# The first matmul of two MLPs as seven half-sized products per 512 hidden columns, with weight sums on VectorE and in accumulating transfers

## The chip, the cores and the metric

One NeuronCore of a Trainium2 chip runs the whole program; the other cores are idle. The metric is the time of one execution on the device in microseconds (us). Five engines work from their own instruction lists: TensorE (PE in the profile, its weight loads PEld), VectorE (DVE), ScalarE (ACT), GpSimd (POOL) and SyncE (SP). SP and POOL issue the transfers (DMAs); only those of POOL add to what lies at the destination (`accum_op=ALU.add`).

## The reference

Two layers on 512 tokens of width 1024, in float32. Each layer is a token mixer (dilated window attention in the first, latent attention in the second) and then an MLP with a hidden width of 4096. The change is about the MLP:

```python
def sq_relu_mlp(h, w1, w2):
    a = jax.nn.relu(h @ w1)
    return (a * a) @ w2

for i in range(DEPTH):
    ...
    x = x + y
    h = rms_norm(x, norm_ffn[i])
    x = x + sq_relu_mlp(h, ffn_w1[i], ffn_w2[i])
```

## The kernel before

Every float32 operand is split in two parts in TensorE's fp32r format: ACT copies it to `hi`, DVE subtracts to get `lo`. A product is then three matmuls: hi·hi, hi·lo and lo·hi. So each weight block costs an ACT copy and a DVE subtraction besides the matmuls.

The MLP stands in `mlp`. `up(ch, grp)` makes 512 of the 4096 hidden columns: four weight units of 128x1024 (`raw`, three buffers, loaded by SP at L147 and split at L157 and L158), 96 matmuls of 512 columns each at L185, and Relu and Square on ACT (L891, L892) into `a2`. Only the first group of a layer runs its matmuls in halves of 256 columns, 192 of them. The normalized tokens stand in `hT_m` as hi and lo, written by `norm_tile` (L228 on ACT, L229 on DVE) while `project`, the output projection of the mixer, still runs for later token tiles.

`down(ch)` takes 1024 hidden columns, in `wino`: seven products in the manner of Strassen and Winograd in place of eight, each of 24 matmuls of 512 columns (L852). Its weight sums need no engine: SP loads a block into a slot of `wqs` (L783) and POOL adds another to it (L781). The sums of the activations are DVE's (L789, into two buffers `S`), their splits L757 and L758 (into four buffers `asp`), and the results are added to the residual at L826. `wqs` takes the space of the big tile `hT` of the mixer, and so waits for the last matmul of `project`.

The order of calls is up(0,0), up(0,1), then for each of three chunks up(ch+1,0), down(ch), up(ch+1,1), and last down(3). A scheduler of the tile framework decides the order on each engine from these calls by its own estimates, and it places waits where a buffer is reused. An engine and a queue work strictly in their order. In the first layer the last `down` also runs the norm for the next mixer, `done0`: its tiles `xn` use the tag and the two buffers of `S`.

Two other places are touched. In the first mixer, `both(4, bT[g], ...)` needs a sum of weights that DVE adds (`add_block`, L334). In the second, the scores (L1114) of the last head pairs run beside the start of `project`.

Of the kernel before, what the change touches and what calls it, by code (L numbers as in the profile page):

```python
# [17 lines left out]
P = 128  # L18
# [69 lines left out]
def encoder_kernel(ctx: ExitStack, tc: tile.TileContext, x, norm_mix, norm_ffn, a_w_qkv, a_q_gain, a_k_gain,  # L88
# [218 lines left out]
    def v_phase(vp):  # L307
# [139 lines left out]
        def piece(g, ba):  # L447
# [11 lines left out]
            add_block(bT[g], bT[g], b21[g])  # L459
# [295 lines left out]
    def split_a(x, pool):  # L755
        t = pool.tile([P, 4, 2, 256], F32R, tag="asp", name=nm("asp"), bufs=4)
        A.activation(t[:, :, 0], x, AF.Copy)  # L757
        V.tensor_tensor(t[:, :, 1], x, t[:, :, 0].bitcast(F32), op=ALU.subtract)  # L758
        return t

    def wino(tag, Aq, w, wqs, pool, resid, done=None):
# [24 lines left out]
        def stmp(name, x, y, op):  # L786
            if name not in S:
                S[name] = pool.tile([P, 4, 256], F32, tag="S", name=nm("S"), bufs=2)
            V.tensor_tensor(S[name], x, y, op=op)  # L789
            return S[name]  # L790
# [14 lines left out]
        b7 = fetch(s7, (1, 1), add=True)  # L805

        def operands(p):
            if p == 5:
                return stmp("c", Aq(1, 0), Aq(1, 1), ALU.subtract), bT
            if p == 1:  # L810
                return Aq(0, 0), b1
            if p == 3:
                stmp("d", S["c"], Aq(0, 0), ALU.subtract)
                return stmp("c", S["d"], Aq(0, 1), ALU.add), b3
            if p == 6:
                return S["d"], fetch(sT, (1, 1), add=True)
            if p == 7:
                return stmp("c", Aq(0, 0), Aq(1, 0), ALU.subtract), b7
# [10 lines left out]

        banks = {}  # L830
        for p, chain, first, (i, n, op) in ORDER if done is None else ORDER_LAST:
            a, wq = operands(p)
            at = split_a(a, pool)
# [20 lines left out]
            put(i, n, op, bk)  # L854


    SLOTS = [(0, 1, 2, 3)]
    for _ in range(3):
# [3 lines left out]
    ORDER = [(1, "a", True, (0, 0, ALU.add)), (5, "b", True, (1, 1, ALU.add)), (3, "b", False, (0, 1, ALU.add)),  # L862
             (6, "a", False, (0, 1, ALU.subtract)), (2, "d", True, (0, 0, ALU.add)),
             (7, "a", False, (1, 1, ALU.subtract)), (4, "a", False, (1, 0, ALU.add))]

    ORDER_LAST = [ORDER[0], ORDER[4]] + ORDER[1:4] + ORDER[5:]

    def mlp(layer, w1, w2, hT_m, resid, pool, done):
        a2s = {}

        wqs = big.tile([P, 8, 2, 512], F32, tag="hT", name=nm("wqs"))

        def up(ch, grp):
            if grp == 0:
                if ch % 2:
                    a2s[ch] = pool.tile([P, 8, S], F32, tag="a2", name=nm("a2"))
                else:
                    a2s[ch] = x16.tile([P, 8, S], F32, tag="x16", name=nm("a2"))
            a2 = a2s[ch]
            c0 = ch * 1024 + grp * 512  # L880
            first = c0 == 0

            def mm(o, kt, hi, lo, hv, n=256 if first else 512):
                wh, wl = hi[:, o * P:(o + 1) * P], lo[:, o * P:(o + 1) * P]
                sl = slice(hv * n, hv * n + n)
                hh, hl = hT_m[:, kt, 0, sl], hT_m[:, kt, 1, sl]
                return [(wh, hh, sl), (wh, hl, sl), (wl, hh, sl)]

            def evac(o, acc):
                f = grp * 4 + o  # L890
                A.activation(a2[:, f], acc, AF.Relu)  # L891
                A.activation(a2[:, f], a2[:, f], AF.Square)  # L892

            run_block(w_units(w1, c0, 512), [4] if first else [1] * 4, 512, mm, evac, halves=2 if first else 1)

        def down(ch):
            a2 = a2s.pop(ch)
            wino(layer * 4 + ch, lambda i, j: a2[:, 4 * j:4 * j + 4, 256 * i:256 * i + 256],
# [4 lines left out]
        for ch in range(3):  # L903
            up(ch + 1, 0)
            down(ch)
            up(ch + 1, 1)
# [320 lines left out]
```

## Time and profile before

| | us |
|---|---|
| median of 3 runs | 1429.62 (1429.39 to 1430.68) |
| the profiled execution | 1427.53 |
| its span in the trace | 1425.8 |

The profiled execution is 2.1 us below the median; its span leaves out 1.7 us around the program.

The page of the profile has the busy time of each engine, the span in 40 slices, the DMA queues, and the chain of work that ended last. It is read here in that order, and then by windows of the trace: the stretch from 549 to 882 us is the MLP of the first layer, and that from 1087 to the end is the MLP of the second. A row of a group of instructions gives line, engine, operation, tile written and read, shape, count, busy time, mean duration in ns and the idle time ahead of it. A row of a window gives its length and the busy time of PE, PEld, DVE, ACT and POOL with their counts, then the granted clock, the share of the DMA engines, and GB/s. A row of the chain gives start, length, engine, tile, line and count. In a row of DMA issues the last number is the median from issue to landing.

| DMA queue | packets | MB | share of 16 engines |
|---|---|---|---|
| SP (q1) | 101808 | 144.96 | 31.6% |
| POOL (q0) | 19184 | 39.07 | 15.2% |

### The profile page before, as it was taken

How to read it: one execution, taken by the hardware profiler on the slowest of the kernel's cores; microseconds unless marked ns; L12 is line 12 of the kernel's file. 1: busy time of each engine (PE TensorE's matmuls, PEld its weight loads, DVE VectorE, ACT ScalarE, POOL GpSimd, SP SyncE). 2: the span in 40 equal slices, each digit the busy share in tenths (PEclk: the TensorE clock that was granted, in tenths of full speed). 3: DMA queues.
4: the chain of work that ended last, by engine and by line, in shares of the span. 5: the costliest groups of instructions: out<-in, count | busy, mean ns of one | idle time of the engine just before them, and what ended most of it. 6: DMA issues, size and time to landing. Idle time of an engine off the chain costs nothing.

```text
span 1425.8 us, 19234 instructions
## 1 busy us (share of the span) xinstructions
PE 1394.0 (98%) x7044; PEld 1183.8 (83%) x7044; DVE 939.6 (66%) x1497; ACT 740.5 (52%) x1594; POOL 217.2 (15%) x240
## 2 busy tenths in 40 slices
PE   7999999999999999999999999999999999999998
PEld 7999888988888988888888887777768888888886
DVE  6886768676886754465564759788745365575647
ACT  6554656464564623553545446677633553544543
POOL 1110212021112001020010203433201020020201
PEclk9999999999999999999999999999999999999999
DMA  9535222322322335668493844200115658394835
GB/s 323 166 134 168 75 87 87 107 89 75 118 61 77 121 134 195 174 133 222 116 233 99 206 120 91 82 31 30 44 40 163 183 127 231 93 234 128 192 90 118
DMA packets 121086, 185.25 MB, mean 130 GB/s; under 512 B 8416, under 2 KB 58336, under 8 KB 120992
## 3 DMA queue, kind: packets, MB, share of 16 engines
q1 hardware_dynamic: 101808, 144.96, 31.6%
q0 software_dynamic: 19184, 39.07, 15.2%
q8 instruction: 55, 0.90, 0.3%
q14 instruction: 39, 0.32, 0.1%
HBM read 176.13 MB, written 7.86 MB: 129 GB/s over the span
## 4 chain that ended last, share of the span: by engine, by line
PE 89%; DVE 6%; ACT 2%; issue 1%; DMA 1%; POOL 0%; SPq 0%; DVEq 0%; ACTq 0%; POOLq 0%
PE acc L185 51%; PE sc L852 11%; PE tp L852 7%; PE tp L124 4%; PE sc L421 3%; PE acc L1138 1%; PE sc L1032 1%; PE acc L1114 1%; PE tp L421 1%; DVE wlo L796 1%; PE sco L701 1%; PE sc L587 1%; PE acc L421 1%; PE sco L697 1%; DVE wlo L407 1%
## 5 line engine op out<-in xcount | busy, mean ns | idle before, releaser
L185 PE MATMUL acc<-whi,hT 128*128 128x512 f32 (+2 forms) x1216 | 384.2, 390 | 2.2 <-ACT hT L739 1.3
L185 PE MATMUL acc<-hT_f,whi 128*128 128x512 f32 (+1 forms) x1152 | 318.7, 366 | 1.7 <-DVE resid L915 1.2
L158 DVE TENSOR_TENSOR wlo<-raw,whi 128x1024 fp32r<-128x1024 f32 (+3 forms) x146 | 172.4, 1189 | 180.2 <-ACT whi L157 179.9
L185 PEld LDWEIGHTS acc<-whi,hT 128*128 128x128 f32 x1216 | 225.4, 188 | 42.0 <-ACT hT L739 1.9
L185 PEld LDWEIGHTS acc<-hT_f,whi 128*128 128x128 f32 x1152 | 208.1, 189 | 37.4 <-DVE resid L915 1.6
L185 PE MATMUL acc<-wlo,hT 128*128 128x512 f32 (+2 forms) x608 | 235.9, 388 | 0.0
L157 ACT ACTIVATE whi<-raw 128x1024 fp32r<-128x1024 f32 (+3 forms) x146 | 149.7, 1031 | 161.5 <-PE acc L185 64.1
L796 DVE TENSOR_TENSOR wlo<-wqs,whi 128x1024 fp32r<-128x1024 f32 x112 | 137.9, 1232 | 113.4 <-ACT whi L795 113.4
L185 PE MATMUL acc<-hT_f,wlo 128*128 128x512 f32 (+1 forms) x576 | 204.9, 366 | 0.0
L795 ACT ACTIVATE whi<-wqs 128x1024 fp32r<-128x1024 f32 x112 | 118.8, 1061 | 161.3 <-PE acc L185 65.8
L852 PE MATMUL sc<-whi,asp 128*128 128x512 f32 x512 | 164.9, 390 | 0.8 <-DVE resid L826 0.7
L781 POOL DMA_DIRECT2D wqs<-in_ffn_w_dram x64 | 77.6, 1344 | 546.1 <-DVE wlo L796 362.4
L185 PEld LDWEIGHTS acc<-wlo,hT 128*128 128x128 f32 x608 | 114.4, 188 | 18.7 <-issue 0.2
L185 PEld LDWEIGHTS acc<-hT_f,wlo 128*128 128x128 f32 x576 | 108.5, 189 | 17.4
L852 PE MATMUL tp<-whi,asp 128*128 128x512 f32 x352 | 112.2, 390 | 1.8 <-DVE resid L826 1.8
L852 PEld LDWEIGHTS sc<-whi,asp 128*128 128x128 f32 x512 | 96.1, 188 | 21.4 <-issue 1.5
L132 POOL TENSOR_TENSOR qrs<-rs_v,nhalf 128x4 f32<-128x4 f32 x48 | 58.7, 1228 | 288.8 <-DVE rs_v L129 239.7
L852 PE MATMUL sc<-wlo,asp 128*128 128x512 f32 x256 | 99.6, 389 | 0.0
L137 ACT ACTIVATE junk<-acc 128x128 f32<-128x128 f32 x192 | 53.0, 276 | 56.4 <-PE acc L185 51.4
L852 PEld LDWEIGHTS tp<-whi,asp 128*128 128x128 f32 x352 | 66.1, 188 | 16.4 <-DVE resid L826 2.7
L852 PE MATMUL tp<-wlo,asp 128*128 128x512 f32 x176 | 68.2, 389 | 0.0
L295 ACT ACTIVATE qkT<-tp 128x512 f32<-128x512 f32 x48 | 35.8, 765 | 51.2 <-PE tp L124 50.9
(231 smaller groups left out, 2185.3 us busy)
## 6 DMA issues: line engine op xcount, KB each, us to landing
wqs<-in_ffn_w_dram SPq DMA_DIRECT2D x80, 512.0 KB, 5.1
raw<-in_ffn_w_dram SPq DMA_DIRECT2D x64, 512.0 KB, 4.5
wqs<-in_ffn_w_dram POOLq DMA_DIRECT2D x64, 512.0 KB, 7.5
raw<-in_a_w_qkv_dram SPq DMA_DIRECT2D x96, 256.0 KB, 3.1
b<-in_a_w_qkv_dram SPq DMA_DIRECT2D x24, 384.0 KB, 5.7
vall<-vo POOLq DMA_DIRECT2D x24, 192.0 KB, 2.2
raw<-in_a_w_o_dram SPq DMA_DIRECT2D x8, 512.0 KB, 3.8
raw<-in_b_w_o_dram SPq DMA_DIRECT2D x8, 512.0 KB, 3.7
```

Of the source, the lines that this page charges most:

```text
L124: PE.transpose(o, i, ident)
L132: G.tensor_tensor(out, v[:, :n], nhalf[:, :n], op=ALU.pow)
L137: A.activation(junk, x, AF.Square, scale=1.0 / math.sqrt(dim), accum_out=out)
L157: A.activation(hi[:, :nk, :n], raw[:, :nk, :n], AF.Copy)
L158: V.tensor_tensor(lo[:, :nk, :n], raw[:, :nk, :n], hi[:, :nk, :n].bitcast(F32), op=ALU.subtract)
L185: PE.matmul(accs[o][:, oc], lhsT=lt, rhs=rt, start=(kt == 0 and p_i == 0 and hv == 0), stop=(kt == total - 1 and p_i == 2), skip_group_che ...
L295: A.activation(dst, tv, AF.Copy)
L421: PE.matmul(banks[t][:, :VH], lhsT=lt, rhs=rt[:, j], start=(first and k == 0 and i_ == 0), stop=(k == 3 and i_ == 2), skip_group_check=True)
L781: marks["sum"] = nc.gpsimd.dma_start(t, src, accum_op=ALU.add).ins
L795: A.activation(hi, x, AF.Copy)
L796: V.tensor_tensor(lo, x, hi.bitcast(F32), op=ALU.subtract)
L852: PE.matmul(bk[t], lhsT=lt, rhs=rt[:, j], start=(first and k == 0 and i_ == 0), stop=(k == 3 and i_ == 2), skip_group_check=True)
```

## The change

The first matmul gets the same treatment as the second. A new class `Up` makes the 512 hidden columns from a 2 by 2 blocking: 256 tokens by 512 inputs by 256 columns, in seven products of 24 matmuls, each of 256 columns (168 in place of 96 of 512). Each product needs one weight operand of 128x1024 and one of seven operands of the tokens. The seven token operands are made once in a layer, in `project`, by the new `norm_blocks`, which takes the place of `norm_tile` there: for the first 256 tokens three transposed blocks or copies, for the others sums and splits (the block `H` of seven takes the place of `hT`). Of the four sums of weights in a group, DVE adds two (for products 5 and 6) and POOL two by accumulating transfers (for 7 and 4). Buffers change too: the block (0,0) of a group gets a pool "wk" of its own with two buffers, `asp` has two buffers in place of four, the sums of `wino` go in halves or through slots "gain" and "wk", and the `xn` of the norm at the end of the first layer's MLP uses the slots "wk" with the sum `d` of product 7. `wino` becomes a generator, whose products are interleaved with those of `Up` by two lists (0 stands for one step of `wino`).

```diff
+        def weight(self, p):
+            w = self.w
+            T = w[0, 0]
+            if p == 5:
+                V.tensor_tensor(T, T, w[0, 1], op=ALU.add)
+            if p == 6:
+                V.tensor_tensor(T, T, w[1, 1], op=ALU.add)
+            if p == 6:
+                self.load((1, 1), w[0, 1], add=True)
+            return w[{3: (1, 1), 7: (0, 1), 2: (1, 0)}.get(p, (0, 0))]
...
+        def product(self, p):
+            x = self.weight(p)
...
+            A.activation(hi, x, AF.Copy)
+            V.tensor_tensor(lo, x, hi.bitcast(F32), op=ALU.subtract)
+            if p == 6:
+                self.load((1, 0), self.w[0, 0], add=True)
...
+            for o in range(2):
+                for k in range(4):
+                    wh, wl = hi[:, k, o * P:(o + 1) * P], lo[:, k, o * P:(o + 1) * P]
+                    for i_, (lt, rt) in enumerate(((wh, H[:, k, 0]), (wh, H[:, k, 1]), (wl, H[:, k, 0]))):
+                        PE.matmul(acc[:, 256 * o:256 * o + 256], lhsT=lt, rhs=rt,
...
+            if p == 1:
+                A.activation(self.block(0, 0), av, AF.Copy)
...
+                V.tensor_tensor(c, c, av, op=op)
+                self.end(c, c)
...
+        g0 = group(0)
+        g0.rest()
+        g0.product(1)
+        g0.product(2)
+        g1 = group(1)
+        g1.product(1)
+        for p in (5, 6, 3, 7, 4):
+            g0.product(p)
+        g1.rest()
...
+            for h, plan in ((2 * ch + 2, (0, 1, 5, 0, 6, 3, 0, 7, 2, 0, 4, 0, 0)),
+                            (2 * ch + 3, (1, 5, 6, 0, 3, 7, 2, 0, 4))):
...
+            if r >= 2:
+                c = dif[:, 0, i]
+                parts_of(5, i, c)
+                V.tensor_tensor(c, c, h32[:, i, 0:4], op=ALU.subtract)
+                parts_of(6, i, c)
+                V.tensor_tensor(c, c, h32[:, i, 4:8], op=ALU.add)
+                parts_of(3, i, c)
+                parts_of(7, i, dif[:, 1, i])
...
-            norm_tile(r, resid[:, r], state["g"], state["hT"], mp, xn_tag="S")
+            norm_tile(r, resid[:, r], state["g"], state["hT"], mp, xn_tag="wk")
```

In the first mixer two of DVE's adds (768 columns each) for one of three head groups become two accumulating transfers of 384 KB. In the second, `project` is not issued before the maximum and the exponential of the eighth score tile from the end:

```diff
+            if g:
+                add_block(bT[g], bT[g], b21[g])
+            else:
...
+                for u in range(2):
+                    nc.gpsimd.dma_start(bT[g][:, 2 * u:2 * u + 2], wblk(g, 1, 0, u), accum_op=ALU.add)
...
+    with tc.tile_pool(name="po1", bufs=1, reuse_waits="tile") as po, \
+            tc.issue_after(last_pair[0]), tc.issue_after(last_pair[1]):
```

Where instructions stand now shows at three places. The first is SP's queue at the start of the first MLP: blocks of w1 go to `raw` (and `wk`), blocks of w2 to `wqs`. Before:

```order
L147 DMA raw_5378<-in_ffn_w_dram 128x2x512
L147 DMA raw_5384<-in_ffn_w_dram 128x2x512
L928 DMA resid<-in_x_dram 128x1024 x4
L147 DMA raw_5390<-in_ffn_w_dram 128x2x512
L147 DMA raw_5396<-in_ffn_w_dram 128x2x512
L783 DMA wqs_5372<-in_ffn_w_dram 128x2x512 x2
L147 DMA raw_5606<-in_ffn_w_dram 128x2x512
L783 DMA wqs_5372<-in_ffn_w_dram 128x2x512
L147 DMA raw_5636<-in_ffn_w_dram 128x2x512
L783 DMA wqs_5372<-in_ffn_w_dram 128x2x512 x5
```

and after:

```order
L924 DMA raw_5406<-in_ffn_w_dram 128x4x256
L924 DMA raw_5408<-in_ffn_w_dram 128x4x256
L1090 DMA resid<-in_x_dram 128x1024 x4
L924 DMA raw_5410<-in_ffn_w_dram 128x4x256
L788 DMA wqs_5400<-in_ffn_w_dram 128x2x512 x8
L924 DMA wk_5404<-in_ffn_w_dram 128x4x256
L924 DMA wk_5474<-in_ffn_w_dram 128x4x256
```

Before, the first four blocks of w1 stood ahead of the eight of w2. Now three do, and the fourth, `wk_5404`, the block (0,0) of the first group, stands behind all eight. The second layer has the same order.

The second place is DVE's list there, from the residual's last add of `project` (L915, now L1077) on; `hT_f` is the operand block of the tokens, `dif` and `h` its sums and copies. Before:

```order
L915 TENSOR_TENSOR resid<-resid,acc_5155 128x512
L229 TENSOR_TENSOR hT_f_5112<-tp_5260,hT_f_5112 128x4x128
L229 TENSOR_TENSOR hT_f_5112<-tp_5267,hT_f_5112 128x4x128
L158 TENSOR_TENSOR wlo_5399<-raw_5396,whi_5398 128x1024
L129 TENSOR_SCALAR rs_v_5349<-nss_5346 128x1
```

and after, the end of the list of the tokens' sums and splits:

```order
L1043 TENSOR_TENSOR hT_f_5112<-dif,hT_f_5112 128x4x128 x3
L1071 TENSOR_TENSOR dif<-dif,h_5118 128x512
L1069 TENSOR_TENSOR dif<-dif,h_5118 128x512
L1043 TENSOR_TENSOR hT_f_5112<-dif,hT_f_5112 128x4x128 x2
L1071 TENSOR_TENSOR dif<-dif,h_5118 128x512
L1043 TENSOR_TENSOR hT_f_5112<-dif,hT_f_5112 128x4x128
L955 TENSOR_TENSOR wlo_5413<-wk_5404,whi_5412 128x1024
```

Before, the weight splits (L158) stood among the norm's instructions and three of them ahead of the last add. Now the first weight split of the MLP, `wlo_5413`, stands behind all of the tokens' 18 instructions that follow the last `xn`.

The third place is DVE's list at the end of the first MLP, where products 6, 7 and 4 of the last `down` run: `sc` are the results of product 6, `a` the activations, `wlo` weight splits of products 7 and 4, `xn` the norm of token tiles 0 and 1, `asp` the split operands. Before:

```order
L758 TENSOR_TENSOR asp_7656<-S_7488,asp_7656 128x4x256
L758 TENSOR_TENSOR asp_7695<-a_1140_6842,asp_7695 128x4x256
L796 TENSOR_TENSOR wlo_7660<-wqs_5372,whi_7659 128x1024
L796 TENSOR_TENSOR wlo_7670<-wqs_5372,whi_7669 128x1024
L826 TENSOR_TENSOR resid<-resid,tp_7494 128x512
L826 TENSOR_TENSOR resid<-resid,sc_7411 128x512
```

and after:

```order
L763 TENSOR_TENSOR asp<-a_955_5403,asp 128x4x256
L823 TENSOR_TENSOR wlo_8392<-wqs_5400,whi_8391 128x1024
L129 TENSOR_SCALAR rs_v_8297<-nss_8294 128x1
L129 TENSOR_SCALAR rs_v_8320<-nss_8317 128x1
L220 SCALAR_TENSOR_TENSOR xn_8295<-resid,nrs_8299,g_mix_1267_8291 128x1024
L220 SCALAR_TENSOR_TENSOR xn_8318<-resid,nrs_8322,g_mix_1267_8291 128x1024
L229 TENSOR_TENSOR hT_8293<-tp_8302,hT_8293 128x4x128
L801 TENSOR_TENSOR d_8339<-a_955_5403 128x1024
L229 TENSOR_TENSOR hT_8293<-tp_8309,hT_8293 128x4x128
L229 TENSOR_TENSOR hT_8293<-tp_8325,hT_8293 128x4x128
L763 TENSOR_TENSOR asp<-d_8339,asp 128x4x256
```

Before, both operands of products 7 and 4 were split ahead of the result of product 6 (`asp_7656`, `asp_7695`). Now these six rows' counterparts are behind the result of product 6 for product 4 (`asp<-a`), and the sum for product 7, `d_8339`, stands behind the norm of both tiles, the first of which, `xn_8295`, has the slot that `d_8339` takes; its split is the last row.

More of the change, by code (lines that the diff above doesn't have):

```diff
@@ L752, in encoder_kernel, with split_to, wino @@
     ap0.__exit__(None, None, None)
[L755 to L756 removed]
+    def split_to(t, x):
         A.activation(t[:, :, 0], x, AF.Copy)
         V.tensor_tensor(t[:, :, 1], x, t[:, :, 0].bitcast(F32), op=ALU.subtract)
[L759 to L761 removed]
+    def wino(tag, Aq, w, wqs, asps, pool, resid, done=None):
         v = w.rearrange("(k p) c -> p k c", p=P)
@@ L860, in encoder_kernel @@
         SLOTS.append((q_, r_, p_, t_))
[L862 to L869, printed above, removed]
-        wqs = big.tile([P, 8, 2, 512], F32, tag="hT", name=nm("wqs"))
[L873 to L876, printed above, removed]
-                else:
[L878 to L898, printed above, removed]
-                 w2[1024 * ch:1024 * ch + 1024, :], wqs, pool, resid, done if ch == 3 else None)
-        up(0, 0)
-        up(0, 1)
[L903 to L906, printed above, removed]
-        down(3)
```

166 lines of the change are left out of this document (146 added, 20 removed).

## The prediction

> **What bounds the kernel now.** The page comes first: the span, the busy times, and the chain of work that ended last.
>
> ```profile
> span 1425.8 us, 19234 instructions
> PE 1394.0 (98%) x7044; PEld 1183.8 (83%) x7044; DVE 939.6 (66%) x1497; ACT 740.5 (52%) x1594; POOL 217.2 (15%) x240
> PE 89%; DVE 6%; ACT 2%; issue 1%; DMA 1%; POOL 0%; SPq 0%; DVEq 0%; ACTq 0%; POOLq 0%
> ```
>
> The reader sees TensorE busy 98% of the span and carrying 89% of the chain, so TensorE is the bound, and matmul time that goes is worth its full length wherever the other engines keep up. The change takes matmuls away and gives the other engines more. So the next view is by windows: one chunk of the first MLP in its steady state, its last chunk, and the first 22 us of each MLP.
>
> ```profile
> 552.90:575.00 22.10, 22.10 (x188) 22.10 (x187) 5.16 (x7) 7.76 (x13) 5.43 (x5) 1.00 1.07 330
> 701.90:783.50 81.60, 81.60 (x362) 67.57 (x361) 47.93 (x47) 39.53 (x46) 9.70 (x8) 1.00 0.67 168
> 843.00:882.00 39.00, 37.40 (x168) 30.46 (x167) 37.69 (x40) 23.50 (x28) 14.43 (x15) 1.00 0.36 61
> 1091.74:1113.84 22.10, 22.10 (x187) 22.10 (x187) 5.09 (x6) 6.90 (x11) 5.42 (x5) 1.00 1.02 297
> ```
>
> The reader sees PE without a gap in a chunk (81.60 of 81.60), with DVE at 47.93/81.60 = 59%; a last chunk in which DVE is at 97% and PE loses 1.6 us; and two starts at which PE is full while the DMA engines are full too (1.07 and 1.02).
>
> **The matmuls.** Their spacing is read in the chain, where nothing else lies between them.
>
> ```profile
> 555.76 2.88 PE acc L185 x24
> 614.88 5.44 PE acc L185 x24
> ```
>
> A matmul of 256 columns takes 2.88/24 = 0.120 us, one of 512 5.44/24 = 0.2267 us. A group of hidden columns took 96 x 0.2267 = 21.76 us, the first of a layer 192 x 0.120 = 23.04; now it takes 168 x 0.120 = 20.16. That is 1.60 x 14 + 2.88 x 2 = **28.2 us less**. On this the Trainium skill has a rule, in "TensorE: Matmul & The Clock Gate", section Back-to-back issue gap: a warm matmul of N columns follows the last after N/2.4 + 2.5 ns. By it the two would be 109 and 216 ns and the saving 38.5 us; the trace has 120 and 227 at a granted clock of 1.00, so each matmul here carries some 13 ns of its own, and the measured 28.2 stands.
>
> **The two starts.** TensorE's first matmul of the MLP needs a block of w1, its split on ACT and DVE, and the tokens' operands. Before, four blocks stood first in SP's queue. Now the block (0,0) stands behind eight blocks of w2, and these wait for the last matmul of the projection, as they did before. The rows are those of SP's queue, with the landing of the first and of a late block, in the first layer and then the second.
>
> ```profile
> 549.23 0.94 SPq L783 DMA_DIRECT2D wqs<-in_ffn_w_dram  x2
> wqs<-in_ffn_w_dram SPq DMA_DIRECT2D x1, 512.0 KB, 5.3
> 554.71 1.16 SPq L783 DMA_DIRECT2D wqs<-in_ffn_w_dram  x1
> wqs<-in_ffn_w_dram SPq DMA_DIRECT2D x1, 512.0 KB, 13.6
> 1087.15 0.88 SPq L783 DMA_DIRECT2D wqs<-in_ffn_w_dram  x2
> wqs<-in_ffn_w_dram SPq DMA_DIRECT2D x1, 512.0 KB, 4.2
> 1091.66 0.45 SPq L147 DMA_DIRECT2D raw<-in_ffn_w_dram  x1
> raw<-in_ffn_w_dram SPq DMA_DIRECT2D x1, 512.0 KB, 14.7
> ```
>
> The first block lands 4.2 to 5.3 us after its issue; the tenth of the first layer (554.71 + 13.6 = 568.3, one more ahead of it than `wk` will have) and the ninth of the second (1091.66 + 14.7 = 1106.4) land some 19 us after the first. At 330 GB/s a block of 524 KB takes 1.59 us, so eight more behind the first give 4.8 + 12.7 = 17.5 us: `wk` lands at **566.7** and **1104.6**. Its split goes ahead of the matmul that uses it.
>
> ```profile
> L157 ACT ACTIVATE whi<-raw 128x1024 fp32r<-128x1024 f32 x128 | 134.9, 1059 | 157.1 <-PE acc L185 63.8 <-PE sc L852 49.1 <-DMA raw<-in_ffn_w_dram 20.6
> L158 DVE TENSOR_TENSOR wlo<-raw,whi 128x1024 fp32r<-128x1024 f32 x128 | 155.5, 1224 | 177.3 <-ACT whi L157 177.0
> 552.92 2.40 PE acc L185 x20
> 558.63 0.44 PE tp L124 x4
> 1091.74 2.39 PE acc L185 x20
> ```
>
> That is 1.06 + 1.22 = 2.28 us, of which two matmuls on the hi part (0.24) lie ahead of the lo part: TensorE is continuous from 568.7 and 1106.6 in place of 552.92 and 1091.74. In between it does three groups of transposes that stood later (0.44 each), while four matmuls that stood before these times are gone (0.5). Cost: 15.8 - 1.3 + 0.5 = 15.0 and 14.9 - 1.3 + 0.5 = 14.1, together **29.1 us**. The window of the start has PE full, so nothing else hides this.
>
> Two bounds. Below: with `wk` at once, its split still stands on DVE behind the tokens' operands, 18 sums and splits like those of this row, one `xn`, two earlier splits and the residual's add.
>
> ```profile
> L229 DVE TENSOR_TENSOR hT_f<-tp,hT_f 128x512 fp32r<-128x512 f32 x16 | 10.6, 686 | 6.2 <-ACT hT_f L228 6.2
> L220 DVE SCALAR_TENSOR_TENSOR xn<-resid,nrs,g_ffn 128x1024 f32<-128x1024 f32 x8 | 10.3, 1283 | 4.0 <-POOL nrs L132 4.0
> 551.01 0.60 DVE resid L915
> ```
>
> From some 549.5, when the last matmul of the projection is done, this is 21 x 0.69 + 1.28 = 15.8 us, then 1.22 for the weights: 566.5 without any wait, or 2.2 us less in each layer: 24.7 together. Above: the late rows as they stand (568.3 and 1106.4) add 1.7 each, and POOL's adds, which come into the same stretch, may add more.
>
> ```profile
> wqs<-in_ffn_w_dram POOLq DMA_DIRECT2D x4, 512.0 KB, 9.6
> 555.91 1.41 SPq L783 DMA_DIRECT2D wqs<-in_ffn_w_dram  x1
> wqs<-in_ffn_w_dram SPq DMA_DIRECT2D x1, 512.0 KB, 16.5
> ```
>
> The block behind the tenth, with two of POOL's adds beside it, landed at 572.4: 5.7 us later than I take, and 11 for both layers, so the starts cost 24.7 to 40. The Trainium skill says, in "DMA: Bandwidth & Descriptors", section Queues, rings and completion order, that a DMA engine takes turns between queues packet by packet. By it an add of POOL halves what is left of SP's queue, which would be some 5 us more in each layer; the tenth block, with adds beside it, landed 1.6 us after where I put the ninth, so I stay with the sum from the blocks.
>
> After the start, sums and reloads of the first two groups have no `down` beside them. A transfer that adds takes 9.6 us and starts when an earlier split is done; the products between cover 4 x 2.88 = 11.5. I take 2 us for both layers (0 to 5).
>
> **The end of the first MLP.** Before, product 7 followed product 6 after a gap of 0.8 us, since its operands were split ahead:
>
> ```profile
> 871.43 0.39 PE L852 MATMUL sc<-whi,asp 128*128 128x512 f32 x1
> 872.49 0.47 PE L852 MATMUL sc<-whi,asp 128*128 128x512 f32 x1 [0.68 <-DVE resid L826]
> L137 ACT ACTIVATE xn<-resid 128x1024 f32<-128x1024 f32 x12 | 12.7, 1058 | 21.5 <-DVE resid L915 21.0 <-DVE resid L826 0.6
> L228 ACT ACTIVATE hT_f<-tp 128x512 fp32r<-128x512 f32 x16 | 9.1, 594 | 17.2 <-PE tp L124 17.2
> ```
>
> Now, from the end of product 6, ACT does two splits (2.1, by L157) and two mean squares (L137, 1.06 and 0.2 for reading the sum out, twice 1.25): 4.6. DVE does two `xn` (2 x 1.28, from 4.8, when both mean squares are in): 7.3. The transposes of the first tile and their split on ACT and DVE (0.59, 0.69) lie beside the second `xn` until 8.0; then come d (1.22, as L158), the ACT split (1.06), and on DVE two more splits (1.4) and that of d (1.22): 11.7. Four matmuls on the hi part (0.9) and 16 transposes of 0.11 that also stood before are no loss: 11.7 - 0.9 - 1.8 - 0.8 = **8 us** (0 if the slot is free earlier, 12 if ACT's splits wait). The second layer's last `down` has no norm.
>
> **The six chunks between.** A group adds on DVE three more splits, two weight sums of the same shape (1.22 each) and three result sums (0.68, by the residual's adds): 8.2 us, 16.3 in a chunk, so 64.2 of 78.4 us, or 82%. What PE does beside a busy DVE shows here:
>
> ```profile
> 400.00:420.00 20.00, 20.00 (x97) 16.68 (x96) 18.31 (x47) 11.82 (x48) 5.27 (x5) 1.00 0.28 84
> 800.00:820.00 20.00, 20.00 (x90) 16.57 (x89) 15.24 (x17) 9.22 (x9) 2.12 (x3) 1.00 1.00 254
> q0 software_dynamic: 19184, 39.07, 15.2%
> ```
>
> At 92% of DVE, and at 76% with the DMA engines full, PE lost nothing; at 97%, in the last chunk, it lost 1.6 in 39 us, which would be 3.2 in a chunk. POOL's queue takes 0.152 x 1425.8/39.07 = 5.5 us of all DMA engines for 1 MB; 2.1 MB more in a chunk make (0.67 x 81.6 + 11.6)/78.4 = 0.85. Nearest are the rows without a loss: I take 0.5 us in a chunk, **3 us** in all (0 to 20).
>
> **The mixers.** In the first, two adds of DVE go, in a stretch where DVE is the bound:
>
> ```profile
> 40.00:60.00 20.00, 18.52 (x106) 17.91 (x105) 20.00 (x25) 10.71 (x17) 3.32 (x5) 1.00 0.45 141
> 50.47 1.82 DVE L334 TENSOR_TENSOR bT<-bT,b 128x768 f32<-128x768 f32 x2
> ```
>
> The gain is at most PE's 1.5 us. The transfers that take their place would land about 9.6 us after 50.5, at 60, and the product that needs them comes at 61; behind them on ACT stand the splits and a copy of the next products. So -1.5 to +3, and I take 0, as for the later start of the projection in the second mixer (-2 to +2): its matmuls still stand between the last scores.
>
> **Sum**, against the profiled 1427.5 us: -28.2 + 29.1 + 2 + 8 + 3 = +13.9, 1441.4. The profiled execution was 2.1 below the median, so the forecast is **1444**.
>
> **Rivals.**
> - *The starts cost half.* The scheduler's order is no time: if the blocks of w2 leave more room and the tokens' operands flow faster, TensorE's first 256-column matmul (L968) comes near 560 and 1098. Then the starts cost 29.1 - 17.3 = 11.8, the sum is -3.4, and the time 1426: faster. It decides from about 562 and 1100 on. Against it speak the full DMA engines in both start windows and the list on DVE, each by itself; for it, that the 18 sums and splits are small. Chance 0.11.
> - *The end of the first MLP is hidden* and the chunks lose nothing: 1444 - 11 = 1433, still slower or just the same. The norm's six steps for the first tile would have to fit beside product 6, whose result they need. Chance 0.11.
> - *Matmuls of 256 columns follow closer* than in the first group of before: every 2 ns less is 168 x 16 x 0.002 = 5.4 us. The row of 24 in 2.88 us is of the same shape and pattern, so 0.03; with 4 ns the time is 1433. By the skill's rule (section Back-to-back issue gap) it would be 1444 - 10 = 1434.
> - *DVE or the DMA engines bind in the chunks*: 3.2 us in each, by the last chunk's row: 1444 + 17 = 1461. For it: 82% and 0.85 are means, and DVE's order mixes the splits of `Up` with those of `wino`, whose operands have two buffers where they had four. Chance 0.15.
> - *As forecast*, 1435 to 1453: 0.60.
>
> Within 0.2% (2.9 us), about what a measurement here can tell from no change, lie 1427 to 1432. Faster takes the first rival and little else: 0.11. Same, from the lower part of the second: 0.09. Slower: 0.80. For 8 in 10 the range runs from 1427 to 1459: it leaves out the first rival and the upper half of the third.
>
> **What would show it.** In the changed profile: L968 at 0.120 us and 24 x 7 in a group; PE idle from about 551 to 568, and in the second layer for as long, ended by the split of `wk` on ACT and DVE, with `wk` landing 17 us after the first `wqs`; PE idle for about 8 us behind product 6 near the end of the first MLP, ended by `asp`; chunks of about 79 us. The prediction is wrong if PE's idle time at the starts is under 8 us, or a chunk is over 81.

## The result, and the profile after

The changed kernel takes 1464.75 us (1464.34 to 1465.66, four runs) beside 1429.51 (1428.83 to 1430.68, four runs) before: a ratio of 1.0247, 95% interval 1.0234 to 1.0261. The forecast was 1444 with a range to 1459. The sign was right, and the loss is 35 us where 14.5 were forecast.

The page of the changed kernel: span, busy times, shares of the chain of work that ended last, the clock granted to TensorE in 40 slices (in tenths), and POOL's queue.

```profile
span 1462.7 us, 21731 instructions
PE 1380.8 (94%) x8004; PEld 1216.5 (83%) x8004; DVE 1079.1 (74%) x1691; ACT 825.0 (56%) x1730; POOL 259.0 (18%) x274
...
PEclk9999999999999996999999998999998899999999
...
q0 software_dynamic: 36624, 56.63, 22.8%
...
PE 82%; DMA 7%; DVE 4%; issue 3%; ACT 3%; SPq 1%; POOL 0%; ACTq 0%; DVEq 0%; POOLq 0%
```

TensorE's busy time fell by 13 us (1394.0 before), yet the span grew by 37: TensorE now stands still. Transfers carry 7% of the chain where they carried 1%, and three stretches have a clock below full speed. The list of what TensorE waited for (in all, times, longest) puts a name to the largest losses:

```profile
PE acc L968 <- ACT whi L954: 32.9, 4, 17.3
...
PE tp L124 <- DVE xn L220: 5.6, 1, 5.6
...
PE sc L1276 <- ACT pe L1281: 2.8, 1, 2.8
```

The first is the split of a weight block at the start of the MLPs, the second the norm at the end of the first MLP, the third a score tile of the second mixer. (A row left out, 8.7 us in the first mixer, stands in the kernel before with 8.4.) To see how much each stage lost, I divide both spans at the first load into `wqs` of each layer, and at the first matmul of the second mixer:

| us | to the first MLP | first MLP | second mixer | second MLP | span |
|---|---|---|---|---|---|
| before | 549.2 | 335.2 | 202.8 | 338.7 | 1425.8 |
| after | 549.8 | 354.0 | 209.6 | 349.3 | 1462.7 |
| difference | +0.6 | +18.8 | +6.9 | +10.6 | +36.9 |
| forecast | 0 | +11.4 | 0 | +2.5 | +13.9 |

The forecast of a row is the share of the sum that falls there, as -14.1 + 15.0 + 1 + 8 + 1.5 for the first MLP. All of the difference lies around a few places. First the two starts, 75 us each, by windows; before, and then after:

```profile
545.00:620.00 75.00, 73.81 (x427) 64.95 (x426) 34.74 (x35) 37.30 (x51) 7.18 (x7) 1.00 0.64 190
1085.00:1160.00 75.00, 72.93 (x423) 64.22 (x422) 34.31 (x33) 37.19 (x51) 6.72 (x7) 1.00 0.65 186
```

```profile
545.00:620.00 75.00, 53.24 (x396) 50.96 (x395) 49.58 (x58) 41.50 (x62) 12.43 (x11) 0.84 0.77 190
1110.00:1185.00 75.00, 54.84 (x408) 52.77 (x408) 50.27 (x59) 43.16 (x64) 12.42 (x11) 0.84 0.79 197
575.00:580.00 5.00, 4.71 (x21) 4.42 (x22) 4.46 (x4) 3.04 (x4) 1.09 (x1) 0.52 0.55 149
1135.00:1140.00 5.00, 3.14 (x13) 2.84 (x14) 3.31 (x3) 2.00 (x2) 0.00 (x0) 0.50 1.07 226
1140.00:1145.00 5.00, 5.00 (x33) 5.00 (x33) 3.23 (x4) 2.60 (x3) 1.29 (x1) 0.70 0.93 195
```

PE is idle for 21.8 and 20.2 us, where it was for 1.2 and 2.1. And when it resumes, it runs at half its clock for some 4 us; busy time times (1 - clock), over the 5-us windows with less than full clock, is another 3.1 and 3.9 us. Less the 1.2 and 2.1 of before, the starts cost 23.6 + 22.0 = **45.6 us** of TensorE's time, against the 29.1 + 2 of the forecast.

The steady stretch is the opposite. One window in each MLP, and then a piece of the chain of work.

```profile
600.00:860.00 260.00, 259.68 (x1692) 238.26 (x1691) 208.32 (x223) 165.10 (x204) 45.59 (x37) 1.00 0.83 193
1182.70:1412.70 230.00, 230.00 (x1472) 210.11 (x1472) 185.55 (x199) 144.22 (x176) 43.06 (x35) 1.00 0.84 191
```

and the piece:

```profile
595.21 24.85 PE acc L968 x205
```

PE lost 0.3 us in 260 and nothing in 230, with DVE at 80% and the DMA engines at 0.83; and a matmul of the new kind takes 24.85/205 = 0.121 us. So the 28.2 us are there. What the starts lose is more than they bring.

The end of the second MLP loses a little too, which the forecast put at nothing. The last 50 us of the span, before and after:

```profile
1375.80:1425.80 50.00, 45.01 (x197) 36.31 (x195) 34.00 (x36) 23.16 (x26) 4.82 (x4) 1.00 0.38 90
```

```profile
1412.70:1462.70 50.00, 43.04 (x198) 34.83 (x196) 35.46 (x43) 19.75 (x22) 4.82 (x4) 1.00 0.48 112
```

PE is idle for 7.0 us where it was for 5.0. No experiment asks why.

### The profile page after: what moved, and what is told of

Same layout as the page of the kernel before. It is cut to its first block, busy times and chain, and to the rows that moved or that the text cites. A ratio compares the mean times of both kernels' runs of the same rounds, so it can differ in the third digit from the quotient of the medians.

```text
span 1462.7 us, 21731 instructions
## 1 busy us (share of the span) xinstructions
PE 1380.8 (94%) x8004; PEld 1216.5 (83%) x8004; DVE 1079.1 (74%) x1691; ACT 825.0 (56%) x1730; POOL 259.0 (18%) x274
## 4 chain that ended last, share of the span: by engine, by line
PE 82%; DMA 7%; DVE 4%; issue 3%; ACT 3%; SPq 1%; POOL 0%; ACTq 0%; DVEq 0%; POOLq 0%
PE acc L185 27%; PE acc L968 19%; PE sc L885 11%; PE tp L885 7%; PE tp L124 3%; DMA wk<-in_ffn_w_dram 3%; PE sc L421 2%; DMA wqs<-in_ffn_w_dram 2%; PE acc L1300 1%; PE acc L1276 1%; PE sc L1194 1%; PE tp L421 1%; PE sco L706 1%; PE sc L592 1%; PE sco L702 1%
## 5 line engine op out<-in xcount | busy, mean ns | idle before, releaser
L968 PE MATMUL acc<-hT_f,whi 128*128 128x256 f32 x1792 | 329.0, 286 | 33.8 <-ACT whi L954 32.9
L968 PEld LDWEIGHTS acc<-hT_f,whi 128*128 128x128 f32 x1792 | 285.5, 194 | 39.0 <-ACT whi L954 34.3
L968 PE MATMUL acc<-hT_f,wlo 128*128 128x256 f32 x896 | 254.4, 285 | 0.0
L968 PEld LDWEIGHTS acc<-hT_f,wlo 128*128 128x128 f32 x896 | 173.4, 194 | 0.0
L158 DVE TENSOR_TENSOR wlo<-raw,whi 128x1024 fp32r<-128x1024 f32 (+3 forms) x82 | 94.3, 1160 | 55.5 <-ACT whi L157 55.3
L157 ACT ACTIVATE whi<-raw 128x1024 fp32r<-128x1024 f32 (+3 forms) x82 | 82.3, 1009 | 57.8 <-PE acc L185 21.9
L955 DVE TENSOR_TENSOR wlo<-wk,whi 128x1024 fp32r<-128x1024 f32 x64 | 78.2, 1224 | 38.6 <-ACT whi L954 38.3
L954 ACT ACTIVATE whi<-wk 128x1024 fp32r<-128x1024 f32 x64 | 67.6, 1059 | 67.7 <-DMA wk<-in_ffn_w_dram 30.2
L955 DVE TENSOR_TENSOR wlo<-raw,whi 128x1024 fp32r<-128x1024 f32 x48 | 58.6, 1224 | 34.7 <-ACT whi L954 32.4
```

The source lines that it names most:

```text
L157: A.activation(hi[:, :nk, :n], raw[:, :nk, :n], AF.Copy)
L158: V.tensor_tensor(lo[:, :nk, :n], raw[:, :nk, :n], hi[:, :nk, :n].bitcast(F32), op=ALU.subtract)
L954: A.activation(hi, x, AF.Copy)
L955: V.tensor_tensor(lo, x, hi.bitcast(F32), op=ALU.subtract)
L968: PE.matmul(acc[:, 256 * o:256 * o + 256], lhsT=lt, rhs=rt, start=(first and o == 0 and k == 0 and i_ == 0), stop=(o == 1 and k == 3 and i ...
```

## The experiments

Each kernel is the changed kernel with one edit unless it says otherwise, and each ratio is to the kernel before.

### Four parts, each by itself

**The order of the second mixer.** `a_no_issue_after` takes away the two waits ahead of `project`:

```diff
-    with tc.tile_pool(name="po1", bufs=1, reuse_waits="tile") as po, \
-            tc.issue_after(last_pair[0]), tc.issue_after(last_pair[1]):
+    with tc.tile_pool(name="po1", bufs=1, reuse_waits="tile") as po:
```

> The changed kernel with the projection of the second mixer issued as before (no issue_after). Theory: in the changed kernel TensorE stands still at 1043 to 1050 us with its clock down, because the projection's matmuls were not let in between the last scores; the second mixer is 7.0 us longer than before. Then the time falls by 5 to 7 us, to 1458-1460. Rival: the 7 us come from the order that the seven token operands force on the norms; then the time stays within 2 us of 1464.8.

1460.59 us, ratio 1.0219 (1.0204 to 1.0234): 4 us less, a little under the 5 to 7 of the theory, and the second mixer takes 204.4 in place of 209.6. The same 20 us ahead of the projection, in the changed kernel and then in this one:

```profile
1036.00:1046.00 10.00, 7.69 (x34) 4.58 (x32) 5.54 (x16) 4.43 (x14) 2.60 (x4) 1.00 0.00 0
1046.00:1056.00 10.00, 8.69 (x33) 7.10 (x34) 9.01 (x18) 6.56 (x11) 0.00 (x0) 0.83 0.46 157
```

```profile
1031.00:1041.00 10.00, 10.00 (x57) 7.95 (x56) 7.93 (x23) 7.42 (x26) 3.44 (x5) 1.00 0.01 2
1041.00:1051.00 10.00, 10.00 (x51) 8.25 (x50) 5.65 (x15) 4.68 (x10) 0.85 (x2) 1.00 0.18 52
```

The projection's matmuls had filled the gaps between the last score tiles, which wait for ACT's exponentials (2.8 us by the list of waits above). Held back, they leave 3.6 us of gaps, and the clock drops (0.83). Without the waits there is none.

**The place of `d` at the end of the first MLP.** `a_own_d` puts it into `a2c`, which is free by then, in place of the slots that it shares with the norm's `xn`:

```diff
-                    d = pool.tile([P, 4, 256], F32, tag="wk", name=nm("d"), bufs=2)
+                    d = spare
...
-                        done if ch == 3 else None)
+                        done if ch == 3 else None, a2c[:, :, 0:256])
```

> The changed kernel with the sum for product 7 of the last down in memory of its own (the third a2, free by then), so that it needs not wait for the norm. Theory: product 7 follows product 6 within 1 us instead of 11.0, and TensorE's clock stays at 1.00: 10 to 11 us less, 1454. Rival: the norm, now beside products 7 and 4, keeps DVE and ACT from the next mixer's first splits and gives half of it back: 1459.

1455.09 us, ratio 1.0181 (1.0166 to 1.0196): 9.7 us less, near the theory. The end of the first MLP, changed kernel and then this one:

```profile
860.00:910.00 50.00, 42.13 (x179) 34.10 (x177) 37.58 (x47) 23.51 (x30) 12.55 (x16) 0.90 0.35 68
```

```profile
860.00:910.00 50.00, 47.09 (x227) 39.60 (x226) 42.55 (x54) 26.67 (x35) 13.10 (x17) 1.00 0.46 98
```

In the changed kernel's list of PE, the first matmul of product 7 is

```profile
894.04 0.79 PE L885 MATMUL sc<-whi,asp 128*128 128x512 f32 x1
```

Product 6 ended at 883.0, 11.0 us earlier (the walk through the norm's steps had 11.7). With `d` in its own place PE's idle time goes from 7.9 to 2.9 us, and the clock stays at 1.00.

**The place of `wk` in SP's queue.** `a_wk_first` issues the loads of the block (0,0) of the first two groups ahead of the eight loads into `wqs`:

```diff
-            for h, plan in ((2 * ch + 2, (0, 1, 5, 0, 6, 3, 0, 7, 2, 0, 4, 0, 0)),
+            if ch == 0:
+                with tc.issue_after(wk_in):
+                    next(d)
+            for h, plan in ((2 * ch + 2, ((0,) if ch else ()) + (1, 5, 0, 6, 3, 0, 7, 2, 0, 4, 0, 0)),
```

> The changed kernel with the first two blocks (0,0) of w1 ahead of the eight of w2 in SP's queue; nothing else moves. Theory: the queue makes the block late, and behind it DVE's list of the tokens' sums and splits is the next bound (done at 566.4 in the changed kernel's trace): first 256-column matmul at 567 to 569 in place of 575.1, and some 9 to 10 us earlier in the second layer, together 16 to 19 us less, 1446-1449. Rival 1: the queue alone binds: first matmul at 553, 40 us less. Rival 2: the block waits for something else: no change.

1463.48 us, ratio 1.0244 (1.0221 to 1.0267): a miss, since the time hardly moves. TensorE does start earlier, as expected, and then stops in the first two groups. From its trace the first matmul of the MLP, with the wait ahead of it:

```profile
566.67 0.79 PE L968 MATMUL acc<-hT_f,whi 128*128 128x256 f32 x2 [8.90 <-ACT whi L954]
```

two adds for product 4, of the first and the second group, in the chain (start, length):

```profile
577.83 10.07 DMA wk<-in_ffn_w_dram
...
600.50 9.63 DMA wk<-in_ffn_w_dram
```

and the 30 us behind the start by windows:

```profile
590.00:600.00 10.00, 7.71 (x50) 7.54 (x50) 6.47 (x7) 6.65 (x10) 1.28 (x1) 0.83 0.79 174
600.00:610.00 10.00, 9.74 (x81) 9.74 (x82) 3.62 (x4) 2.88 (x4) 1.28 (x1) 1.00 0.80 191
610.00:620.00 10.00, 7.59 (x60) 6.97 (x59) 8.08 (x9) 7.62 (x11) 1.28 (x1) 1.00 0.44 103
```

The matmul came at 575.1 in the changed kernel, so 8.5 us are won; most of them are lost again behind the transfers that add for product 4, which take 10 us from issue to landing. When the first one is issued, at 577.8, PE has work until 590.0. The transfer lands at 587.9, but its split on ACT and what stands behind that split on DVE take until 592.0, and PE waits 2.1 us for DVE.

**POOL's adds beside the loads.** `a_adds_late` leaves SP's queue as it is and holds the first four adds into `wqs` until the first group's own adds are issued:

```diff
+            if ch == 0:
+                with tc.issue_after(g0_add):
+                    next(d)
```

> The changed kernel with POOL's four first adds into wqs held behind the first group's first adding transfer; SP's queue stays. Theory: these adds took the DMA engines' time from SP's queue, so the block (0,0) landed 24 us (first layer) and 27 us (second) after the first block of w2 instead of the 17.5 of the prediction. Then it lands 17 to 19 us after it, and the time falls by 10 to 15 us, to 1450-1455. Rival: the blocks' 1-KB runs are slow by themselves: it lands as late as now, and the time stays or rises.

1463.56 us, ratio 1.0240 (1.0225 to 1.0256): a miss by the time. The first split of `wk`, in the changed kernel and then in this one; the number in brackets is the idle time of ACT ahead of it and what ended it:

```profile
574.02 1.06 ACT L954 ACTIVATE whi<-wk 128x1024 fp32r<-128x1024 f32 x1 [8.32 <-DMA wk<-in_ffn_w_dram]
```

```profile
566.36 1.06 ACT L954 ACTIVATE whi<-wk 128x1024 fp32r<-128x1024 f32 x1 [0.66 <-DMA wk<-in_ffn_w_dram]
```

and one window of this one, behind the start:

```profile
590.00:600.00 10.00, 7.18 (x47) 6.98 (x46) 5.36 (x6) 4.73 (x6) 1.28 (x1) 0.83 1.13 226
```

`wk` is there 16.5 us after the first `wqs` was issued (549.8) in place of 24.2; in the second layer it is there 15.1 us after in place of 22.1. So four adds of POOL, of half a megabyte each, had held up SP's block by 7.7 and 7.0 us, though they were issued 3 us and more behind it. That agrees with the Trainium skill on this point ("DMA: Bandwidth & Descriptors", section Queues, rings and completion order: an engine takes turns between queues). But again the time isn't won: PE stops at 590, as above.

### Behind the first block: sums or clock?

Two kernels ask what sets the first groups. `b_wk_first_dve` is `a_wk_first` with the sums for products 7 and 4 of the first two groups on DVE in place of transfers:

```diff
-            if p == 6:
+            if p == 6 and self.c0 >= 1024:
                 self.load((1, 1), w[0, 1], add=True)
+            if p == 7 and self.c0 < 1024:
+                V.tensor_tensor(w[0, 1], w[0, 1], w[1, 1], op=ALU.add)
+            if p == 4 and self.c0 < 1024:
+                V.tensor_tensor(T, T, w[1, 0], op=ALU.add)
```

> As a_wk_first, and the two weight sums of groups 0 and 1 that went by accumulating transfers are DVE's (no transfers for them; the other 14 groups as in the change). Theory: in a_wk_first the 8 us won at each start were given back in the first two groups, where a sum by transfer takes 10 us from its issue and only two products stand between (5.8 us), and TensorE then lost 5 us and ran at a lower clock behind each stall. Then these stalls go: 5 to 7 us in each layer, 1450-1453. Rival: the blocks of w1 themselves are late there, behind the eight of w2: no more than 3 us less, 1460.

1453.28 us, ratio 1.0174 (1.0159 to 1.0189): 10 us less than `a_wk_first`, at the upper end of the theory. The two windows with stops are now:

```profile
590.00:600.00 10.00, 8.81 (x69) 8.40 (x70) 8.84 (x9) 7.96 (x11) 0.00 (x0) 1.00 0.01 3
610.00:620.00 10.00, 10.00 (x76) 9.60 (x75) 8.50 (x10) 7.97 (x13) 1.28 (x1) 1.00 0.70 158
```

`b_dummy_clock` keeps TensorE busy through the wait instead, with 130 matmuls at each start whose results nobody reads (added work):

```diff
+        idle = acc_p.tile([P, 512], F32, tag="acc", name=nm("acc"))
+        for n in range(130):
+            PE.matmul(idle[:, 0:256], lhsT=H[:, H_OF[4], 0, 0, P:2 * P], rhs=H[:, H_OF[1], 0, 0],
+                      start=(n == 0), stop=(n == 129), skip_group_check=True)
```

> The changed kernel with 130 matmuls of 256 columns without a use at the start of each MLP, behind the tokens' transposes and ahead of the first product; the wait for the block stays. Theory: TensorE's clock falls to 0.5 in a wait of many us and comes back some 4 us after work does, which costs 2 us behind each wait; with TensorE kept busy the first products run at 0.120 us a matmul from the first on, and the time falls by 2 to 4 us, to 1461-1463. Rival: the slow first matmuls come from the operands (DVE and ACT still splitting, the DMA engines full), not from the clock: 0.21 us a matmul stays and the time too, or rises.

1468.86 us, ratio 1.0288 (1.0267 to 1.0310): slower by 4, a miss. The clock does what was expected, the time doesn't:

```profile
575.00:580.00 5.00, 5.00 (x44) 5.00 (x43) 3.90 (x5) 2.49 (x3) 1.30 (x1) 1.00 0.61 165
590.00:595.00 5.00, 2.76 (x18) 2.55 (x17) 1.07 (x1) 1.54 (x2) 0.00 (x0) 0.83 0.62 209
```

At 575 the products now run at full clock (0.52 in the changed kernel), and what they gain they wait for at 590. The wait and what ends it, on PE and on ACT:

```profile
592.73 0.50 PE L968 MATMUL acc<-hT_f,whi 128*128 128x256 f32 x2 [2.24 <-ACT a L975]
591.13 1.06 ACT L954 ACTIVATE whi<-wk 128x1024 fp32r<-128x1024 f32 x1 [3.32 <-DMA wk<-in_ffn_w_dram]
```

PE waits for ACT's copy of an earlier result (`a`, L975), which stands on ACT behind the split of the block that an adding transfer brings. The same rows of the changed kernel:

```profile
595.21 0.50 PE L968 MATMUL acc<-hT_f,whi 128*128 128x256 f32 x2 [0.21 <-ACT a L977]
593.61 1.06 ACT L954 ACTIVATE whi<-wk 128x1024 fp32r<-128x1024 f32 x1 [3.74 <-DMA wk<-in_ffn_w_dram]
```

There the slow matmuls fill nearly all of that wait. So in the changed kernel the half clock at the start can't be won back by itself: it lies beside the chain from `wk` through sum, split and transfer. Why the whole is 4 us slower was not resolved.

### The parts together, and an earlier start

`b_three_fixes` takes `a_no_issue_after`, `a_own_d` and `b_wk_first_dve` together.

> All edits that theory asks for, at once: no issue_after, the first blocks (0,0) ahead of w2 in SP's queue, DVE sums in groups 0 and 1, and memory of its own for the sum of product 7. If they are independent their gains add: -4, -9.4 and -12 to -15 from 1464.7: 1436-1439, 0.5% slower than before. If they overlap (a wait behind each): 1445 or more.

1439.29 us, ratio 1.0067 (1.0050 to 1.0084). The three gains alone, 4.2 + 9.7 + 11.5, make 25.4; together 25.5: they lie at different places and add, as the theory had it.

What is left at the starts is, by the theory, the wait for the operands of the tokens. `b_early_products` moves three products that need only the first 256 tokens (two of the first group, one of the second) ahead of the norm of the last token tile:

```diff
+        def run(self):
...
+            g0.product(1)
+            g0.product(2)
+            g1.product(1)
...
+                if c == 1 and r == 3:
+                    norm_blocks(2)
+                    early()
+                    norm_blocks(3)
```

> As b_three_fixes, and the first three products (1 and 2 of group 0, 1 of group 1), which need only token tiles 0 and 1, stand ahead of the sums and splits of tile 3 on DVE and ACT. Theory: what is left of the starts is DVE's list of the tokens' operands; then TensorE starts near 552 and the tokens' list costs 3 to 5 us in place of 15 in each layer: 1415-1425, faster than before. Rival: the list moves behind the weight splits and TensorE waits for it after three products as long as it did ahead of them: 1432-1438.

1435.82 us, ratio 1.0049 (1.0034 to 1.0064): a miss, inside the rival's range. Its start by windows:

```profile
560.00:565.00 5.00, 5.00 (x44) 4.92 (x43) 4.27 (x8) 2.53 (x5) 1.19 (x1) 1.00 1.08 270
565.00:570.00 5.00, 1.92 (x14) 1.55 (x13) 5.00 (x8) 3.21 (x7) 1.21 (x1) 1.00 1.13 206
570.00:575.00 5.00, 2.22 (x15) 1.72 (x13) 5.00 (x7) 4.35 (x6) 0.00 (x0) 0.87 0.59 107
575.00:580.00 5.00, 2.15 (x10) 2.15 (x11) 4.62 (x5) 1.69 (x2) 0.00 (x0) 0.50 0.67 208
```

PE works from 555 to 565 and then waits 8.7 of 15 us, with DVE full. Three kernels on top of it look for the rest. `c_nrs_first` holds POOL's adds behind the norm factor of the last tile, which stood behind one of them; `c_pool_sums` adds to that the sums for products 7 and 4 on GpSimd's own compute; `c_no_v_part` is `c_nrs_first` with the edit of the first mixer undone.

> b_early_products with POOL's adds into wqs held behind the norm factor (nrs) of the last token tile. There nrs (L132) stood on POOL behind an add that waited for a DMA and came about 5 us late in both layers, while TensorE waited 9 and 14 us for the token operands. Theory (the token operands of the last tile set the end of the start, and nrs holds them): 3 to 4 us less in each layer, 1428 to 1431. Rival (VectorE's list of token sums and splits, full from 565 to 580 us, sets it whatever nrs does): within 2 us of 1435.8.

> c_nrs_first with the weight sums of products 7 and 4 in the first two groups of each layer on GpSimd's own compute in place of VectorE. Theory (VectorE's list is the bound of the start): four sums of 1.22 us leave it in each layer, 3 to 8 us less than c_nrs_first in all, so 1423 to 1428. Rival (GpSimd's sum of 128x1024 is slow, and holds up what is queued behind it, and product 7 waits for it): slower than c_nrs_first by 3 to 10 us, 1432 to 1440.

> c_nrs_first with the edit in the first mixer undone alone: both late weight sums of the first head group are VectorE's again. The prediction put this edit at nothing (-1.5 to +3); by the ledger the stretch up to the MLP is 0.6 us longer in the changed kernel. Theory: within 1 us of c_nrs_first, with the stretch to the first wqs issue 0.6 us shorter. Rival (the edit gains): 1 to 1.5 us slower.

1435.40, 1437.15 and 1435.79 us; ratios 1.0048 (1.0033 to 1.0063), 1.0056 (1.0039 to 1.0072) and 1.0049 (1.0034 to 1.0064). The first follows its rival, and the third its theory: the first mixer's edit is worth nothing that can be measured. In the second the theory falls (1.7 us slower, with intervals that overlap). So the factor was not the point. On DVE's four sums the test says less: GpSimd takes 2.4 to 3.3 us for each where DVE takes 1.2. PE's wait for the tokens' operands is as long in both (14.8 + 6.4 us below, and 15.7 + 5.5). In `c_nrs_first` the factor is 2 us earlier, and yet DVE then stands idle for 3.2 us, since the transposes of that tile stand on PE behind a product that runs at half clock (0.53 from 555 to 560). The factor on POOL is

```profile
555.54 0.55 POOL L132 TENSOR_TENSOR nrs<-rs_v,nhalf 128x1 f32<-128x1 f32 x1 [8.94 <-DVE rs_v L129]
```

and, on DVE, what waits for the copy (`dif`, ACT) of those transposes:

```profile
560.60 0.69 DVE L1097 TENSOR_TENSOR dif<-tp,dif 128x512 f32<-128x512 f32 x1 [3.20 <-ACT dif L1094]
```

### Eight products in the first group

The method needs sums of tokens and of weights before it can go on; a plain product needs none. `d_plain_first` is `c_nrs_first` with the first group of each layer as eight plain half-sized products (four blocks of weights, each split once and used for both halves of the tokens), 2.88 us more of matmuls. Here `run` issues the four products of the first 256 tokens (`row(0, n)`) and `second` the other four (`row(1, n)`); the sums of tokens (`norm_sums`) go behind the two splits that these need:

```diff
+        def row(self, i, n):
+            acc = self.banks[i, n] = acc_p.tile([P, 512], F32, tag="acc", name=nm("acc"))
+            for q, kk in enumerate((1, 0) if i else (0, 1)):
+                hi, lo = self.parts[kk, n]
...
                     norm_blocks(2)
-                    early()
+                    early.run()
                     norm_blocks(3)
+                    early.second()
+                    norm_sums(0)
+                    norm_sums(1)
```

> c_nrs_first with the first 512 hidden columns of each layer by eight plain half-sized products (192 matmuls of 256 columns, 2.88 us more than by seven), whose four weight blocks need no sums; the first four of them need the operands of the first 256 tokens alone, and the other four only two splits of the last 256 tokens, so that the sums of tokens stand behind those splits on VectorE, beside the products. Theory (what the change costs is the time until all token and weight sums are there; in the steady state its 28.2 us are whole): in c_nrs_first TensorE waits 10 us between 545 and 610 us and runs some 15 us at a granted clock of 0.5 to 0.8, about 6 us more; of these 16 us in each layer 10 to 13 go, less 2.9 for the eighth product: 1415 (1411 to 1420), faster than before by 0.6 to 1.2%. Rival (VectorE's list for the last token tile, or its transposes behind a product, still hold up the second half of the group and then the group behind it): 2 to 4 us less in each layer, 1427 to 1432, no faster than before.

1421.92 us (1419.44 to 1423.65), ratio **0.9946** (0.9933 to 0.9960): 13.5 us less than `c_nrs_first`, and faster than the kernel before. It came out 2 us above the theory's range and 5 below the rival's. The starts:

```profile
545.00:620.00 75.00, 70.41 (x528) 67.43 (x527) 58.61 (x69) 49.15 (x73) 10.98 (x10) 0.98 0.71 184
1080.00:1155.00 75.00, 69.50 (x523) 66.74 (x522) 58.57 (x69) 48.85 (x73) 10.96 (x10) 0.98 0.70 183
550.00:555.00 5.00, 2.18 (x11) 1.73 (x10) 4.34 (x8) 3.76 (x7) 0.55 (x1) 0.81 0.98 315
```

PE's idle time in these 75 us is 4.6 and 5.5, where it was 21.8 and 20.2 in the changed kernel; most of what is left of the first lies between 550 and 555. The waits of PE for the tokens' operands, in `c_nrs_first` and then here (us in all, times, longest):

```profile
PE acc L972 <- DVE hT_f L1076: 14.8, 8, 3.5
PE acc L972 <- ACT hT_f L1075: 6.4, 6, 1.8
```

```profile
PE acc L1025 <- DVE hT_f L1109: 4.6, 4, 2.1
PE acc L1025 <- ACT hT_f L1108: 4.0, 4, 1.6
```

The run doesn't part the plain products from the later place of the tokens' sums, which they make possible.

## Why the prediction was off

The sign was right. The size of the largest term, the starts, was not, and two stretches that were put at nothing lost 6.9 and 2.0 us.

**The matmuls: right.** 0.120 us was put down for one, and 24.85/205 = 0.121 measured; the steady stretch is full. The rule that the prediction cites beside this stands in the same section of the Trainium skill as the gap of an isolated matmul, so it wasn't made for a stream like this one.

**The two starts: the size of the term was wrong, 29.1 + 2 forecast and 45.6 measured.** This is two thirds of the error of 23 us (36.9 - 13.9, by spans), and it has two parts.
- *"so I stay with the sum from the blocks"* failed. `wk` was put 17.5 us behind the first `wqs`; it landed at 574.0, 24.2 us behind. In the second layer the first `wqs` is issued at 1113.4, and the split of `wk` starts, as soon as it has landed, 22.2 us behind:

```profile
1135.60 1.06 ACT L954 ACTIVATE whi<-wk 128x1024 fp32r<-128x1024 f32 x1 [6.28 <-DMA wk<-in_ffn_w_dram]
```

  `a_adds_late` shows the cause: without POOL's adds it lands 16.5 and 15.1 us behind the first `wqs`, so the blocks were counted about right, and the adds beside them were not counted at all. The upper bound had named them at 11 us for both layers, and 6.7 + 4.7 = 11.4 is what they came to; the Trainium skill's rule on queues gave some 5 in each layer.
- The clock was left out, and with it 3.1 + 3.9 us: when PE resumes after the wait it has 0.50 of its clock for some 4 us.

The two make more than the 14.5 us that were missing, since the forecast didn't take off the 3.3 us that the kernel before loses in the same windows. They are not gains to be had one by one: `a_adds_late` and `b_dummy_clock` each take one away, and the time stays or rises, since PE then waits for the adding transfers of the first groups.

The step *"the products between cover 4 x 2.88 = 11.5"* held in the changed kernel: its stops there are 0.2 us, and 0.7 in the second layer (1155 to 1160 us), inside the 2 that were forecast. Where the first products come earlier (`a_wk_first`) or run at full clock (`b_dummy_clock`), it fails. What it leaves out is that the split of product 4's block stands on ACT or DVE ahead of results of earlier products, so that PE stops before product 4. `b_wk_first_dve`, in which the same sums on DVE bring 10 us, shows what that is worth once the block is early.

**The end of the first MLP: right in mechanism, 8 forecast.** By the windows of 860 to 910 us PE lost 7.9 us idle and 3.3 of clock (three windows of 5 us are below full clock), less the 1.6 that it lost there before: 9.6. Undone, it gave 9.7.

**The six chunks: 3 forecast, 0.3 measured**, in the windows of 260 and 230 us. The rows without a loss, at 92% of DVE, were the right ones to read.

**The second mixer: 0 forecast (-2 to +2), +6.9 measured.** The step that failed is *"its matmuls still stand between the last scores"*. The order showed that some do; it didn't show that those which fill the first gaps were gone. `a_no_issue_after` returns 5.2 of the 6.9 by the same division of its span, 4 by the median. The other 1.7 us were not traced.

**The end of the second MLP: 0 forecast, +2.0 measured**, by the last 50 us of both spans. *"The second layer's last `down` has no norm"* is so, and something else costs there; the cause stays open.

**The first mixer: 0 forecast, +0.6 by the table.** `c_no_v_part` finds nothing to tell from zero.

Sum: -28.2 + 45.6 + 9.6 + 0.3 + 6.9 + 2.0 + 0.6 = +36.8, beside a span that grew by 36.9. The rival *DVE or the DMA engines bind in the chunks*, which gave nearly the measured time (1461), is not what happened. *The starts cost half* was tried from the other side: with `d_plain_first`, which has the other edits too, they cost little, and the time is below the kernel before.

## What to carry to other kernels

A method that saves work per group can need more things ready before its first group than the plain one does: price the first group by itself, from the landing of its last operand, and let it run the plain way if that is cheaper. Count every queue that moves bytes into the same stretch, also those issued later by another engine. On ACT and DVE an instruction that waits for a transfer held up what stood behind it, so look there too for what a late transfer stops. A matmul that fills gaps elsewhere isn't free to move: ask what stands in the gap it leaves.

## What was not expected of the hardware

- Adding transfers of 512 KB on POOL's queue, issued 3 us and more after a plain load of the same size on SP's, delayed it by 7.7 us (landed at 574.0 with them, at 566.3 without).
- After 17.3 us without work TensorE ran 256-column matmuls 0.213 us apart for about 4 us, at a granted clock of 0.50, and then 0.120 apart. The Trainium skill describes the gate in "TensorE: Matmul & The Clock Gate", Part 1, with an idle window of some 3.4 us ahead of the slow state; the long waits agree with that. So does the gap of 5.6 us at the end of the first MLP (product 7 then ran at 0.43 us for a matmul of 512 columns until 897). A shorter gap was enough too: after the 2.24 us at 590 in `b_dummy_clock` the matmuls stood 0.213 us apart until 597, so the measured gap, and not the 3.4 us, is what to go by here.
